# The triangular inverses of a chunked RWKV-7 recurrence: rows spread over the partitions, and one strict mask instead of two

## Chip, core and metric

One core of one Trainium2 chip runs the whole kernel in one launch. The metric is the device time of an execution in microseconds. Of three runs of the kernel before the median is 1870.58 us (1870.54 to 1880.12).

## What is computed

One layer of a decoder trunk on 1024 tokens of 1024 channels, all in float32: an input projection feeds a sparse attention, an RWKV-7 time mixing and two gates; then come a cross-attention and a mixture of experts with their norms. The part that matters here is the time mixing, with 8 heads of 64 channels. The reference runs it token by token:

```
def step(S, inp):
    r_t, w_t, k_t, v_t, kk_t, a_t = inp
    S = (S * w_t[:, :, None, :]
         - jnp.einsum('bhij,bhj->bhi', S, kk_t)[..., None] * (kk_t * a_t)[:, :, None, :]
         + v_t[..., None] * k_t[:, :, None, :])
    return S, jnp.einsum('bhij,bhj->bhi', S, r_t)
```

## The kernel before, in words

**The stage.** The input projection multiplies blocks of 128 weight columns with the 1024 tokens, each as three matmuls of split operands (lines 35 to 37: high by high, low by high, high by low). While these run, class Rwkv works through 8 items: 4 pairs of heads (hp) by 2 halves of 512 tokens (n). The string ORDER (line 1784) gives the order in which projection blocks of the recurrence ("r"), items ("i") and the other projection blocks ("b") are written; all items stand before the first "b". The framework then plans the order of each engine's instructions from a simulated timeline (line 1913), so the engines' queues interleave items with projections. Every engine runs its queue in order; a late operand holds up all that is behind it.

**An item** (`steps`, line 704) cuts the 512 tokens into 8 chunks of 64 for each of 2 heads. A pair of chunks shares a 128 x 128 tile, so there are 8 units u (2 heads by 4 pairs).

- Line 805: products of decayed keys and factors, four per bank of the PSUM tag tp, two banks' worth in use.
- Lines 809 to 814, for each of 4 banks: four instructions on 32 partitions cut the strictly triangular 32 x 32 diagonal blocks into lx (line 811), then three instructions on 128 partitions by 256 elements make f, lk and lo with the masks 0, 1 and 2. lk holds the strict triangles of the key half only; the other half of its 128 rows is zero. lo holds the off-diagonal 32 x 32 blocks.
- Line 836: per unit one product of lk with the values vt, 128 rows by 128 columns by 64, into rr.
- Lines 842 to 848: the blocks lx go to a memory tile ld (four stores) and come back as ln (four loads), so that each of the 32 blocks (8 units by 4) lies in one partition, four times: partition group g of 32 works on 8 of the 32 rows of each inverse.
- Lines 849 to 852: the inversion by substitution, 31 steps of two VectorE instructions, all over 8 rows and 31 - j elements. Group g holds rows 8g to 8g + 7; the identity is loaded into x first (line 846).
- Lines 855 to 859: the inverses x go to memory (xd, four stores), and come back as diagonal blocks of dt (four loads).
- Lines 866 to 881: for each head, TensorE applies dt, lo and dt again (line 870, its rhs is rr, z or qq in turn), with copies and sums on VectorE (z at line 873, w at 878, yv at 881) and ScalarE (qq at 876) between.
- Lines 885 to 894: products of f with w in 64 x 64 form (line 891), into gp.
- Lines 898 to 910: the chain over 8 chunks (lines 903 and 905, copies of the state at 909). Norm and gate follow in the next item's time (lines 913 to 939).

All transfers are issued on SyncE's queue, in its order: the four ld stores, the identity, the four ln loads, the four xd stores and the four dt loads of an item, between the weights' loads (line 114) and the evictions of the projections. A float32 product with float32 operands appears as two TensorE instructions in the profile, so line 836 has 16 per item.

Of the kernel before, what the change touches and what calls it, by code (L numbers as in the profile page):

```python
# [11 lines left out]
ALU = mybir.AluOpType  # L12
# [7 lines left out]
class Ctx:  # L20
    def __init__(self, tc, a):
        self.tc, self.nc, self.a = tc, tc.nc, a
        self.s = {}
# [587 lines left out]
def host_consts3():  # L611
    r = np.arange(128)[:, None] % 64
    t = np.arange(64)[None, :]
    lo_half = (np.arange(128) < 64)[:, None]
    incl, strict = (r <= t), (r < t)
    off = (r < 32) & (t >= 32)
    mk = np.zeros((4, 128, 2, 64), np.float32)
    for par in range(2):
        beta = lo_half if par == 0 else ~lo_half
        mk[0, :, par] = np.where(incl, np.where(beta, -1.0, 1.0), 0.0)  # L620
        mk[1, :, par] = strict & ~beta
        mk[2, :, par] = -1.0 * (off & beta)
        mk[3, :, par] = strict
    blk = (np.arange(128)[:, None] // 64 == np.arange(128)[None, :] // 64).astype(np.float32)
    sm = np.ones((128, 512), np.float32)
    sm[:, ::64] = 0
    return {"c_rmask": np.ascontiguousarray(mk.transpose(1, 0, 2, 3)), "c_blk": blk, "c_scan": sm,
            "c_i64": np.concatenate([np.eye(64, dtype=np.float32)] * 2, 0),
            "c_i32": np.repeat(np.eye(32, dtype=np.float32).reshape(4, 256), 32, 0)}


class Rwkv:
# [5 lines left out]
    def __init__(self, k, cst, dp, p1, pb, ps):  # L638
        self.k, self.cst, self.dp, self.p1, self.pb, self.ps = k, cst, dp, p1, pb, ps
        nc, a, s = k.nc, k.a, k.s  # L640
        s["or"], s["bo"] = ([dp.tile([128, T], F32, name=f"{n}{b}") for b in range(4)] for n in ("or", "bo"))

        def cload(name, shape, src):
            t = p1.tile(shape, F32, name=name)
            nc.sync.dma_start(t, src)
            return t
        self.rmask = cload("rmask", [128, 4, 2, 64], a["c_rmask"])
        self.blk = cload("blk", [128, 128], a["c_blk"])
        self.scan = cload("scan", [128, 512], a["c_scan"])
        self.i64 = cload("i64", [128, 64], a["c_i64"])  # L650
        vec = {}
        for n in ("w0", "a0", "kk", "ka", "gn_g", "gn_b"):
            vec[n] = cload("v" + n, [128, 4], a["rwkv_" + n][0].rearrange("(b p) -> p b", p=128))
        vec["rk"] = cload("vrk", [128, 4], a["rwkv_rk"][0].rearrange("(b h) d -> (h d) b", h=2))
        for n in ("w0", "a0"):
            nc.vector.tensor_scalar(vec[n], vec[n], 0.5, None, ALU.mult)
        vec["ka2"] = p1.tile([128, 4], F32, name="ka2")
        nc.vector.tensor_scalar(vec["ka2"], vec["ka"], -0.5, 1.0, ALU.mult, ALU.add)
        nc.vector.tensor_scalar(vec["ka"], vec["ka"], 0.5, None, ALU.mult)
        self.vec = vec  # L660
        self.mhalf = p1.tile([128, 8], F32, name="mhalf")
        nc.vector.memset(self.mhalf, -0.5)
        self.last, self.marks = (), {}
        self.dt = p1.tile([128, 8, 128], F32, name="dt")
        nc.gpsimd.memset(self.dt, 0.0)
        self.st = [p1.tile([128, 128], F32, name=f"state{i}") for i in range(2)]
        for t in self.st:
            nc.gpsimd.memset(t, 0.0)
# [35 lines left out]
    def steps(self, hp, n):  # L704
        k, nc, s, pb, ps, dp = self.k, self.k.nc, self.k.s, self.pb, self.ps, self.dp
        ident, rmask = self.cst["ident"], self.rmask
# [4 lines left out]
        def bank(tag="acc", bufs=2):  # L711
            return ps.tile([128, 512], F32, tag=tag, bufs=bufs, name="r" + tag)

        def big(tag, shape=(128, W), bufs=1):
            return pb.tile(list(shape), F32, tag=tag, bufs=bufs, name="r_" + tag)
# [24 lines left out]
        acc = bank("pa", 1)  # L740
        nc.tensor.matmul(acc, wa2[0:64], zwa[0:64], start=True, stop=True)
        nc.scalar.activation(th, acc, AF.Tanh, bias=v1["w0"], scale=0.5)
        acc = bank("pa", 1)
# [10 lines left out]
        acc = bank("pa", 1)  # L754
# [8 lines left out]
        acc = bank("pa", 1)  # L763
# [27 lines left out]
        acc = bank("pa", 1)  # L791
# [2 lines left out]
        nc.sync.dma_start(s["bo"][hp][:, ns], kx)  # L794

        f = big("f", (128, 2, 8, 2, 64), 3)
        lk, lo, lx = big("lk", (128, 8, 128)), big("lo", (128, 8, 128), 2), big("lx", (128, 8, 32))
        for h in range(2):
            rows = slice(64 * h, 64 * h + 64)
            for q in range(2):  # L800
                acc = bank("tp", 2)
                for i in range(4):
                    c = 4 * q + i
                    lhs = bk[rows, c // 2, 2 * (c % 2):2 * (c % 2) + 2, :].rearrange("p a t -> p (a t)")
                    nc.tensor.matmul(acc[:, 128 * i:128 * i + 128].rearrange("p (a t) -> p a t", a=2), lhs, ar[rows, 0:2, 64 * c:64 * c + 64], start=True, stop=True)
                a5 = acc.rearrange("p (c l x t) -> p c l x t", c=2, l=2, x=2)
                mb = lambda m: rmask[:, m].unsqueeze(1).to_broadcast([128, 2, 2, 64])
                us = slice(4 * h + 2 * q, 4 * h + 2 * q + 2)
                for b in range(4):
                    p2, t2 = slice(32 * b, 32 * b + 32), slice(32 * (b % 2), 32 * (b % 2) + 32)  # L810
                    nc.vector.tensor_tensor(lx[p2, us], a5[p2, :, b // 2, 0, t2], rmask[p2, 3, 0:1, t2].to_broadcast([32, 2, 32]), ALU.mult)
                nc.vector.tensor_tensor(f[:, h, 4 * q:4 * q + 4, 0, :].rearrange("p (c l) t -> p c l t", l=2), a5[:, :, :, 1, :], mb(0), ALU.mult)
                for m, dst in ((1, lk), (2, lo)):
                    nc.vector.tensor_tensor(dst[:, us].rearrange("p c (l t) -> p c l t", l=2), a5[:, :, :, 0, :], mb(m), ALU.mult)

        rr = big("rr", (128, 2, 8, 64))
        vt = big("vt", (128, 4, 2, 64))
# [15 lines left out]
            nc.scalar.copy(vt[h2], a4[o2])  # L833
        acc = bank("tp", 2)
        for u in range(8):
            nc.tensor.matmul(acc[:, 64 * u:64 * u + 64], lk[:, u], vt[:, u % 4, u // 4], start=True, stop=True)
        nc.scalar.copy(rr[:, 1], acc.rearrange("p (u i) -> p u i", i=64))

        ld = dp.tile([8, 4, 32, 32], F32, tag="ld", bufs=2, name="ld")
        xd = dp.tile([8, 4, 32, 32], F32, tag="xd", bufs=2, name="xd")  # L840
        for b in range(4):
            nc.sync.dma_start(ld[:, b].rearrange("u s t -> s u t"), lx[32 * b:32 * b + 32])

        ln = pb.tile([128, 32, 32], F32, tag="ln", name="ln")
        x, tmp = (pb.tile([128, 8, 32], F32, tag=m, name=m) for m in ("xinv", "tinv"))
# [1 line left out]
        for g in range(4):  # L847
            nc.sync.dma_start(ln[32 * g:32 * g + 32].rearrange("p s t -> p (s t)"), ld.rearrange("u b s t -> (u b) (s t)"))
        for j in range(31):
            w = 31 - j  # L850
            nc.vector.tensor_tensor(tmp[:, :, :w], x[:, :, j:j + 1].to_broadcast([128, 8, w]), ln[:, j:j + 1, j + 1:].to_broadcast([128, 8, w]), ALU.mult)  # L851
            nc.vector.tensor_tensor(x[:, :, j + 1:], x[:, :, j + 1:], tmp[:, :, :w], ALU.subtract)  # L852
        xv = xd.rearrange("u b (g s) t -> g (u b) (s t)", g=4)
        for g in range(4):
            nc.sync.dma_start(xv[g], x[32 * g:32 * g + 32].rearrange("p s t -> p (s t)"))
        dt = self.dt
        for b in range(4):
            bs = slice(32 * b, 32 * b + 32)
# [2 lines left out]
        w = big("w", (128, 8, 64))  # L861
# [4 lines left out]
        for h in range(2):  # L866
# [12 lines left out]
            for par in range(2):  # L879
                p2 = slice(64 * par, 64 * par + 64)  # L880
# [4 lines left out]
        for par in range(2):  # L885
            p2 = slice(64 * par, 64 * par + 64)
            acc = bank()
            for i in range(4):
                c = par + 2 * i
# [8 lines left out]
        for c in range(8):  # L898
            op = slice(64 * (c % 2), 64 * (c % 2) + 64)
            st, sn = self.st[c % 2], self.st[1 - c % 2]  # L900
            acc = bank("seq", 1)
# [24 lines left out]
        acc = bank()  # L926
# [9 lines left out]
        acc = bank()  # L936
# [536 lines left out]
class Experts:  # L1473
# [194 lines left out]
    def list(self, r, s0):  # L1668
        main = self.rows(self.pl, s0, "m")
        return main, self.rows(self.pl, s0 + CAP, "r", True) if r < NREM else None  # L1670
# [224 lines left out]


_CONSTS = [host_consts, host_consts2, host_consts3, host_consts5]


# [19 lines left out]
```

## Time and profile before

| what | value |
|---|---|
| median of three runs | 1870.58 us |
| the profiled execution | 1872.08 us |
| its span, first to last instruction | 1870.3 us |
| mean granted TensorE clock | 0.964 |
| busy TensorE / VectorE / ScalarE / GpSimd | 93% / 68% / 45% / 29% |

The granted clock is a share of 2.4 GHz, with two levels in this profile, 1.0 and 0.5. Busy time is the union of an engine's instructions. A wait is idle time of an engine directly ahead of an instruction, put down to what released it last. The recurrence occupies about the stretch from 150 to 650 us.

### The profile page before, as it was taken

How to read it: one execution, taken by the hardware profiler on the slowest of the kernel's cores; microseconds unless marked ns; L12 is line 12 of the kernel's file. 1: busy time of each engine (PE TensorE's matmuls, PEld its weight loads, DVE VectorE, ACT ScalarE, POOL GpSimd, SP SyncE). 2: the span in 40 equal slices, each digit the busy share in tenths (PEclk: the TensorE clock that was granted, in tenths of full speed). 3: DMA queues.
4: the chain of work that ended last, by engine and by line, in shares of the span. 5: the costliest groups of instructions: out<-in, count | busy, mean ns of one | idle time of the engine just before them, and what ended most of it. 6: DMA issues, size and time to landing. Idle time of an engine off the chain costs nothing. (4 is left out here: it accounts for less than half of the span.)

```text
span 1870.3 us, 27135 instructions
## 1 busy us (share of the span) xinstructions
PE 1744.0 (93%) x9126; PEld 1423.5 (76%) x9126; DVE 1277.4 (68%) x2866; ACT 845.5 (45%) x1756; POOL 535.9 (29%) x681
## 2 busy tenths in 40 slices
PE   8999998999999899999999789999998999999992
PEld 6877777777687787878888567878797888888871
DVE  3226876888877621489888575647887777777786
ACT  4233313433333222188888441015313676676672
POOL 1124202221211121166756222100015333333214
PEclk9999999999999899999999899999988999999996
DMA  7363343444432225811200675131433999998974
GB/s 232 113 187 109 108 167 117 131 131 121 112 109 80 78 85 172 275 57 39 84 10 21 200 232 189 46 99 52 162 135 125 326 291 298 294 306 299 310 273 152
DMA packets 245629, 296.01 MB, mean 158 GB/s; under 512 B 55597, under 2 KB 143685, under 8 KB 244976
## 3 DMA queue, kind: packets, MB, share of 16 engines
q1 hardware_dynamic: 238016, 273.59, 44.6%
q0 software_dynamic: 7472, 20.67, 4.5%
q8 instruction: 73, 1.20, 0.3%
q14 instruction: 68, 0.56, 0.1%
HBM read 231.95 MB, written 70.98 MB: 162 GB/s over the span
## 5 line engine op out<-in xcount | busy, mean ns | idle before, releaser
L35 PE MATMUL acc<-xh,wh 128*128 128x512 f32 (+1 forms) x656 | 272.6, 416 | 5.4 <-ACT wh L117 2.5
L37 PE MATMUL acc<-xh,wl 128*128 128x512 f32 (+1 forms) x656 | 266.8, 408 | 0.2 <-POOL wl L118 0.2
L36 PE MATMUL acc<-xl,wh 128*128 128x512 f32 (+1 forms) x656 | 266.2, 406 | 0.0
L1530 DVE TENSOR_TENSOR wlo<-wraw,whi 128x512 fp32r<-128x512 f32 x384 | 237.4, 683 | 30.0 <-ACT whi L1529 30.0
L1529 ACT CAST whi<-wraw 128x512 fp32r<-128x512 f32 x384 | 206.3, 621 | 19.2 <-issue 16.6
L118 POOL TENSOR_TENSOR wl<-wraw,wh 128x1024 fp32r<-128x1024 f32 (+1 forms) x41 | 100.9, 2462 | 304.4 <-ACT wh L117 250.8
L35 PEld LDWEIGHTS acc<-xh,wh 128*128 128x128 f32 (+1 forms) x656 | 125.1, 191 | 43.5 <-issue 5.5
L37 PEld LDWEIGHTS acc<-xh,wl 128*128 128x128 f32 (+1 forms) x656 | 124.5, 190 | 33.3 <-issue 4.7
L36 PEld LDWEIGHTS acc<-xl,wh 128*128 128x128 f32 (+1 forms) x656 | 124.7, 190 | 29.7 <-issue 3.2
L851 DVE TENSOR_TENSOR tinv<-xinv,ln 128x248 f32<-128x248 f32 (+30 forms) x248 | 91.4, 368 | 41.8 <-DMA ln<-ld 16.6
L475 ACT ACTIVATE pp<-pp,nm 128x640 f32<-128x640 f32 (+7 forms) x128 | 94.2, 739 | 9.3 <-DVE nm L474 8.1
L28 DVE TENSOR_TENSOR pl<-ptp,ph 128x512 fp32r<-128x512 f32 x132 | 87.3, 684 | 11.9 <-ACT ph L28 11.3
L35 PE MATMUL eacc<-whi,exh 128*128 128x512 f32 x240 | 94.2, 392 | 0.0
L36 PE MATMUL eacc<-wlo,exh 128*128 128x512 f32 x240 | 94.1, 392 | 0.0
L37 PE MATMUL eacc<-whi,exl 128*128 128x512 f32 x240 | 93.9, 391 | 0.0
L1638 POOL DMA_INDIRECT accd<-ey,ef x32 | 52.6, 1642 | 141.6 <-ACT ey L1633 60.1
L480 POOL TENSOR_SCALAR pp<-pp,wgt 128x640 f32<-128x640 f32 (+7 forms) x128 | 88.2, 715 | 0.6
L852 DVE TENSOR_TENSOR xinv<-xinv,tinv 128x248 f32<-128x248 f32 (+30 forms) x248 | 83.4, 336 | 5.9
L980 POOL TENSOR_SCALAR lnrs<-lnmv 128x1 f32<-128x1 f32 x21 | 18.0, 859 | 223.5 <-DVE lnmv L979 204.5
L28 ACT CAST ph<-ptp 128x512 fp32r<-128x512 f32 x132 | 73.8, 583 | 16.8 <-PE ptp L534 16.0
L534 PE MATMUL ptp<-ident,pp 128*128 128x128 f32 x528 | 79.2, 276 | 0.4 <-DVE pl L28 0.3
L909 ACT COPY state<-rseq 64x64 f32<-64x64 f32 x128 | 26.7, 208 | 115.9 <-PE rseq L905 96.8
(498 smaller groups left out, 4414.7 us busy)
## 6 DMA issues: line engine op xcount, KB each, us to landing
wraw<-in_moe_w_up SPq DMA_DIRECT2D x32, 1024.0 KB
wraw<-in_moe_w_gate SPq DMA_DIRECT2D x32, 1024.0 KB
wraw<-in_moe_w_down SPq DMA_DIRECT2D x32, 1024.0 KB
wraw<-in_w_in SPq DMA_DIRECT2D x40, 512.0 KB
sm<-ev SPq DMA_DIRECT2D x32, 256.0 KB
sr<-ev SPq DMA_DIRECT2D x28, 256.0 KB
skew<-skew SPq DMA_DIRECT2D x1, 4608.0 KB
xraw<-in_x SPq DMA_DIRECT2D x8, 512.0 KB
```

Source lines behind the costliest of these rows:

```text
L28: x = nc.scalar.copy(hi, src), (nc.gpsimd if by_pool else nc.vector).tensor_tensor(lo, src, hi.bitcast(F32), ALU.subtract)
L35: nc.tensor.matmul(out, ah, bh, start=start, stop=False)
L36: nc.tensor.matmul(out, ah, bl, start=False, stop=False)
L37: nc.tensor.matmul(out, al, bh, start=False, stop=stop)
L118: nc.gpsimd.tensor_tensor(wl, raw, wh.bitcast(F32), ALU.subtract)
L475: nc.scalar.activation(pt[:, :n], pt[:, :n], AF.Exp, bias=nm, scale=-1.0, accum_out=sums[:, 0, i:i + 1])
L480: nc.gpsimd.tensor_scalar(st[br, i][:, :n], st[br, i][:, :n], w[:, 0, i:i + 1], 1.0, ALU.mult, ALU.mult)
L534: nc.tensor.transpose(tp[:, 128 * i:128 * i + 128], st[br, i][:, c0:c0 + 128], ident)
L851: nc.vector.tensor_tensor(tmp[:, :, :w], x[:, :, j:j + 1].to_broadcast([128, 8, w]), ln[:, j:j + 1, j + 1:].to_broadcast([128, 8, w]), ALU ...
L852: nc.vector.tensor_tensor(x[:, :, j + 1:], x[:, :, j + 1:], tmp[:, :, :w], ALU.subtract)
L1529: nc.scalar.copy(hi[:, cs], raw[:, cs])
L1530: (nc.gpsimd if i in LOPOOL else nc.vector).tensor_tensor(lo[:, cs], raw[:, cs], hi[:, cs].bitcast(F32), ALU.subtract)
```

## The change

1. The inversion. Partition group g now holds rows g, g + 4, g + 8, ... of each inverse (the identity constant is laid out accordingly). At step j only rows up to j can have a nonzero element in column j, so only the first m = j // 4 + 1 rows held per partition are touched. The stores of xd write rows of 32 elements at a step of four rows.
2. The masks. Mask 1 becomes the full strict triangle; lx, its four instructions per bank and mask 3 go. lk, now first of three, serves both the keys' product and the blocks stored to ld.
3. The keys' product. As the other half of lk is no longer zero, line 836's product becomes two per unit, each with 64 rows and 64 columns.

```
-    mk = np.zeros((4, 128, 2, 64), np.float32)
+    mk = np.zeros((3, 128, 2, 64), np.float32)
...
-        mk[1, :, par] = strict & ~beta
+        mk[1, :, par] = strict
         mk[2, :, par] = -1.0 * (off & beta)
-        mk[3, :, par] = strict
...
-            "c_i32": np.repeat(np.eye(32, dtype=np.float32).reshape(4, 256), 32, 0)}
+            "c_i32": np.repeat(np.eye(32, dtype=np.float32).reshape(8, 4, 32).transpose(1, 0, 2).reshape(4, 256), 32, 0)}
...
-        lk, lo, lx = big("lk", (128, 8, 128)), big("lo", (128, 8, 128), 2), big("lx", (128, 8, 32))
+        lk, lo = big("lk", (128, 8, 128)), big("lo", (128, 8, 128), 2)
...
-                for b in range(4):
-                    p2, t2 = slice(32 * b, 32 * b + 32), slice(32 * (b % 2), 32 * (b % 2) + 32)
-                    nc.vector.tensor_tensor(lx[p2, us], a5[p2, :, b // 2, 0, t2], rmask[p2, 3, 0:1, t2].to_broadcast([32, 2, 32]), ALU.mult)
-                nc.vector.tensor_tensor(f[:, h, 4 * q:4 * q + 4, 0, :].rearrange("p (c l) t -> p c l t", l=2), a5[:, :, :, 1, :], mb(0), ALU.mult)
                 for m, dst in ((1, lk), (2, lo)):
                     nc.vector.tensor_tensor(dst[:, us].rearrange("p c (l t) -> p c l t", l=2), a5[:, :, :, 0, :], mb(m), ALU.mult)
+                nc.vector.tensor_tensor(f[:, h, 4 * q:4 * q + 4, 0, :].rearrange("p (c l) t -> p c l t", l=2), a5[:, :, :, 1, :], mb(0), ALU.mult)
...
-            nc.tensor.matmul(acc[:, 64 * u:64 * u + 64], lk[:, u], vt[:, u % 4, u // 4], start=True, stop=True)
+            for l in range(2):
+
+                ls, ks = slice(64 * l, 64 * l + 64), slice(64 - 64 * l, 128 - 64 * l)
+                nc.tensor.matmul(acc[ls, 64 * u:64 * u + 64], lk[ks, u, ls], vt[ks, u % 4, u // 4], start=True, stop=True)
...
-            nc.sync.dma_start(ld[:, b].rearrange("u s t -> s u t"), lx[32 * b:32 * b + 32])
+            nc.sync.dma_start(ld[:, b].rearrange("u s t -> s u t"), lk[32 * b:32 * b + 32, :, 32 * b:32 * b + 32])
...
-            w = 31 - j
-            nc.vector.tensor_tensor(tmp[:, :, :w], x[:, :, j:j + 1].to_broadcast([128, 8, w]), ln[:, j:j + 1, j + 1:].to_broadcast([128, 8, w]), ALU.mult)
-            nc.vector.tensor_tensor(x[:, :, j + 1:], x[:, :, j + 1:], tmp[:, :, :w], ALU.subtract)
-        xv = xd.rearrange("u b (g s) t -> g (u b) (s t)", g=4)
+            w, m = 31 - j, j // 4 + 1
+            nc.vector.tensor_tensor(tmp[:, :m, :w], x[:, :m, j:j + 1].to_broadcast([128, m, w]), ln[:, j:j + 1, j + 1:].to_broadcast([128, m, w]), ALU.mult)
+            nc.vector.tensor_tensor(x[:, :m, j + 1:], x[:, :m, j + 1:], tmp[:, :m, :w], ALU.subtract)
+        xv = xd.rearrange("u b (s g) t -> g (u b) s t", g=4)
         for g in range(4):
-            nc.sync.dma_start(xv[g], x[32 * g:32 * g + 32].rearrange("p s t -> p (s t)"))
+            nc.sync.dma_start(xv[g], x[32 * g:32 * g + 32])
```

## Rows read from the trace of the kernel before

**Rows 1.** The page, part 1: busy us of each engine (share of the span) xinstructions.
```profile
PE 1744.0 (93%) x9126; PEld 1423.5 (76%) x9126; DVE 1277.4 (68%) x2866; ACT 845.5 (45%) x1756; POOL 535.9 (29%) x681
```

**Rows 2.** Busy us by stretch: PE, PEld, DVE, ACT, POOL, then PEclk, DMA share, GB/s.
```profile
150.00:650.00 500.00, 468.23 (x2645) 373.18 (x2645) 393.97 (x1049) 169.19 (x366) 108.87 (x82) 0.96 0.38 115
...
655.00:790.00 135.00, 132.18 (x712) 109.62 (x711) 37.07 (x77) 31.18 (x73) 25.88 (x13) 1.00 0.59 182
```

**Rows 3.** TensorE's waits, 150 to 650 us: line <- released by: total us, times, longest.
```profile
PE racc L870 <- DVE r_z L873: 6.7, 5, 1.9
PE racc L870 <- DMA dt<-xd: 5.5, 3, 2.7
PE racc L891 <- DVE r_w L878: 4.8, 1, 4.8
PE rpa L765 <- DVE r_cs L761: 4.7, 3, 2.7
...
PE rtp L805 <- DVE r_lo L814: 1.1, 1, 1.1
PE rtp L822 <- DVE xinv L852: 1.0, 1, 1.0
...
PE acc L35 <- DVE ev L199: 0.9, 1, 0.9
```

**Rows 4.** VectorE's groups, 150 to 650 us: xcount, busy us, mean ns, idle before.
```profile
L851 DVE TENSOR_TENSOR tinv<-xinv,ln 128x248 f32<-128x248 f32 (+30 forms) x248 | 91.4, 368 | 41.8 <-DMA ln<-ld 16.6 <-DMA sm<-ev 8.4 <-DMA sks1h<-ev 7.5
L852 DVE TENSOR_TENSOR xinv<-xinv,tinv 128x248 f32<-128x248 f32 (+30 forms) x248 | 83.4, 336 | 5.9
L811 DVE TENSOR_TENSOR r_lx<-rtp,rmask 32x64 f32<-32x64 f32 x128 | 28.0, 218 | 7.0 <-PE rtp L805 5.1
```

**Rows 5.** VectorE's timeline at 183 and from 630 us: start us, us, instruction.
```profile
183.15 0.42 DVE L851 TENSOR_TENSOR tinv<-xinv,ln 128x248 f32<-128x248 f32 x1 [1.33 <-DMA ln<-ld]
...
630.60 2.42 DVE L851 TENSOR_TENSOR tinv<-xinv,ln 128x72 f32<-128x72 f32 x1
...
639.17 0.17 DVE L852 TENSOR_TENSOR xinv<-xinv,tinv 128x8 f32<-128x8 f32 x1
```

**Rows 6.** Busy us of three stretches at half clock, columns as in rows 2.
```profile
431.40:434.80 3.40, 3.40 (x15) 3.21 (x15) 2.56 (x7) 1.17 (x2) 0.00 (x0) 0.50 0.56 106
509.90:513.30 3.40, 3.40 (x12) 2.79 (x10) 3.25 (x12) 1.59 (x3) 0.80 (x1) 0.50 0.32 95
...
632.70:646.40 13.70, 10.75 (x49) 7.73 (x49) 7.51 (x27) 1.34 (x4) 0.23 (x1) 0.50 0.21 53
```

**Rows 7.** TensorE's timeline beside them; the brackets give the wait before.
```profile
431.13 1.26 PE L870 MATMUL racc<-r_z,r_lo 128*128 128x128 f32 x5 [0.97 <-DVE r_z L873]
...
508.44 1.16 PE L870 MATMUL racc<-r_z,r_lo 128*128 128x128 f32 x8 [1.85 <-DVE r_z L873]
...
635.65 1.97 PE L891 MATMUL racc<-r_f,r_w 64*64 64x128 f32 x14 [4.81 <-DVE r_w L878]
```

**Rows 8.** TensorE's timeline at 192 and 257 us: lines 836 and 891, merged runs.
```profile
192.23 1.90 PE L836 MATMUL rtp<-r_vt,r_lk 128*128 128x64 f32 x16
...
257.17 0.39 PE L36 MATMUL acc<-xl,wh 128*128 128x512 f32 x1
257.40 0.40 PE L37 MATMUL acc<-xh,wl 128*128 128x512 f32 x1
257.73 1.58 PE L891 MATMUL racc<-r_f,r_w 64*64 64x128 f32 x30
```

**Rows 9.** SyncE's timeline: the trip of ld at 483 us, of xd at 524 us.
```profile
483.66 1.85 SPq L842 DMA_DIRECT2D ld<-r_lx  x4
486.74 1.71 SPq L848 DMA_DIRECT2D ln<-ld  x4
...
524.07 1.72 SPq L855 DMA_DIRECT2D xd<-xinv  x4
...
526.99 1.80 SPq L859 DMA_DIRECT2D dt<-xd  x4
```

More of the change, by code (lines that the diff above doesn't have):

```diff
@@ L646, in cload @@
             return t
-        self.rmask = cload("rmask", [128, 4, 2, 64], a["c_rmask"])
+        self.rmask = cload("rmask", [128, 3, 2, 64], a["c_rmask"])
         self.blk = cload("blk", [128, 128], a["c_blk"])
```

## The prediction

> **What bounds the kernel now.** The engine totals come first [rows 1]: TensorE is busy 93% of the span, VectorE 68%. Averages hide the stages, so I next read the stretch in which the recurrence runs, 150 to 650 us, beside the one behind it, where the same projections go on without the inversions [rows 2]. In the first TensorE is busy 468.2 of 500 us, idle 31.8 us or 6.4%, with VectorE at 394 us; in the second it is idle 2.8 of 135 us, 2.1%, with VectorE at 37 us. So TensorE bounds both, and what the recurrence can still give is the idle time that it causes, not its own length. The waits of TensorE say who ends that idle time [rows 3]: the six rows that name a VectorE result (r_z, r_w, r_cs, r_lo, the inversion, an eviction) sum to 6.7 + 4.8 + 4.7 + 1.1 + 1.0 + 0.9 = 19.2 us; the block inverses coming back from memory (dt) make 5.5 us. VectorE's groups show what stands in its queue [rows 4]: the two instructions of the inversion take 91.4 + 83.4 = 174.8 us and the lx masks 28.0 us, 203 of its 394 us, nearly all of it waited for by nobody but the recurrence itself.
>
> **The inversion.** Its 62 instructions per item stay; their sizes fall. Step j now runs over j // 4 + 1 rows of 31 - j elements instead of 8 rows. Summed over the 31 steps that is 1560 elements instead of 8 x 496 = 3968. One instruction of 248 elements took 0.42 us, one of 8 took 0.17 [rows 5]: 0.25 us for 240 elements, 1.04 ns each, on a fixed part of about 0.16 us. Saved per item: 2 x 2408 x 1.04 ns = 5.0 us, over 8 items 40 us. By the same line the old inversions should have taken 8 x (62 x 0.16 + 7936 x 0.00104) = 145 us; the other 30 us of the 174.8 are instructions that stalled, as the one of 72 elements that took 2.42 us where the line gives 0.23 [rows 5]. I leave those stalls in.
>
> **The masks.** The 128 lx instructions go: 28.0 us [rows 4]. The lk and lo masks keep their size, the f mask only moves behind them. Together VectorE loses 40 + 28 = 68 of 394 us in this stretch; its load falls from 0.79 to 326 / 500 = 0.65.
>
> **What TensorE gets of it.** None of this is TensorE work, so the 68 us count only through the 19.2 us of waits. Bounds: nothing, since the order on each engine is planned from assumed durations and a plan with shorter inversions can place the dependent matmuls earlier by as much; and all 19.2 us. In between I take a queue estimate: an instruction that arrives at a server with load u waits in proportion to u / (1 - u), 3.76 before and 1.86 after, half. As the plan will use up some of this, I take 40%: 7.7 us. It lies nearer the estimate than to nothing because the largest wait is just this: TensorE stood 4.81 us before the w product [rows 7] while VectorE worked through steps of the inversion, one of them stalled [rows 5].
>
> Some of these waits have a second price. Stretches in which TensorE was granted half its clock (1.2 of 2.4 GHz) begin right behind or inside a VectorE wait at 431.4, 509.9 and 632.7 us [rows 6, 7]. In them TensorE was busy 3.40 + 3.40 + 10.75 = 17.6 us, which at full clock is 8.8 us of work, so they cost 8.8 us. If 40% of their causes go, 3.5 us goes. Bounds: nothing, and 8.8 us.
>
> **The keys' product.** One product with 128 rows becomes two of 64 rows and 64 columns: 32 instructions per item instead of 16. The old ones came every (1.90 - 0.28) / 15 = 0.108 us, and the nearest rows to the new form, the 64 x 64 products of line 891, every (1.58 - 0.27) / 29 = 0.045 us [rows 8]. So 32 x 0.045 = 1.4 us stands against 16 x 0.108 = 1.7 us. From the last projection matmul to the first 64 x 64 one passed 257.73 - 257.40 = 0.33 us, where two projections followed each other after 0.23 [rows 8]; two such 0.1 us per item eat the difference. I take zero. Bounds: -0.3 us per item, and 32 x 0.108 - 1.7 = +1.8 us per item, 14 us in all, if the pairs do not overlap. The Trainium skill (TensorEngine Tiling (Array Packing), Key Properties) speaks against the change here: it says that a change of the tiling mode drains the engine. It gives no size, so by it the sum would only be worse; by the rows it is 8 x 2 x 0.1 = 1.6 us against 2.4 us gained, so the drain is seen and is small.
>
> **The transfers.** ld now leaves from lk: still 32 partitions x 8 runs of 128 bytes per store, as the block is 32 elements wide; zero. The stores now wait for the last lk instead of the last lx; lk is the first of three masks behind each bank, about 0.42 us as an instruction of this size took [rows 5], where four lx of 0.22 us stood first [rows 4], so they start no later. xd is written as runs of 128 bytes instead of 1 KB per partition, 256 runs a store. The nearest rows are the ld stores, which have these runs: from the end of their four issues to the first load behind them passed 486.74 - (483.66 + 1.85) = 1.23 us; for the 1 KB runs of xd 526.99 - (524.07 + 1.72) = 1.20 us, and issuing four took 1.85 against 1.72 us [rows 9]. So about 0.1 to 0.2 us per item, on the path from an inversion to dt. It is covered by projection matmuls where TensorE has them planned before line 870; the cover is gone where TensorE already waits for dt, three times now [rows 3], so under 0.5 us: zero. Behind the stores on SyncE's queue stand dt's loads and weights, shifted by the same 0.1 us. The smaller mask load and the lost lx tile cost nothing: no wait names either.
>
> **The sum.** -7.7 - 3.5 = -11.2 us. The profiled execution took 1872.1 us (span 1870.3), 1.5 us above the median of the runs, 1870.6; the terms apply to either, so the forecast is 1870.6 - 11.2 = 1859.
>
> **Rivals.**
> - *No change.* VectorE was not the bound and the plan spends the shorter inversions: TensorE's DVE waits stay near 19 us, with other names. For it: the order of work is planned, and TensorE is 94% busy. Against it: half of VectorE's work in this stretch shrinks, and the waits come where its queue is long. Time about 1868, between 1863 and 1873.
> - *Slower: dt takes the place.* The plan puts line 870's products earlier because the inversion is shorter, but the two trips through memory stay, so TensorE stands for dt in all 8 items instead of 3. Price: five more waits of the longest now, 2.7 us [rows 3], each followed by a half-clock stretch of 3.4 us like those of [rows 6], 1.7 us lost: 5 x 4.4 = 22 us, less the 11 gained: 1881. It decides from three such items on. Against it: the trips measured with 128 byte runs are no longer than with 1 KB. The Trainium skill (DMA: Bandwidth & Descriptors, Specifications) speaks for it: transfers under 512 bytes are read-modify-written and lose line rate; by it the trips lengthen and this rival comes, by [rows 9], where no such difference shows, the forecast does.
> - *Far more.* All VectorE waits go, and the half-clock stretches with them: -19.2 - 8.8 = -28 us, 1843. For it, the waits are short, mean 1 to 2 us. Against it, stalls like the 2.42 us one remain.
> - *The pairs do not overlap* (+14 us): 1859 + 14 = 1873. Against it: 0.045 us on line 891.
>
> **How the numbers follow.** A measurement of this kernel can tell about 0.5%, 9.4 us, from no change: faster is below 1861.2, slower above 1880. Forecast 0.42 (1852 to 1865; 0.36 of it counts as faster), no change 0.22, slower by dt 0.18 (0.14 of it above 1880), far more 0.12, no overlap 0.06. Faster 0.36 + 0.12 = 0.48; same 0.06 + 0.22 + 0.04 + 0.06 = 0.38; slower 0.14. The likeliest case by itself spans 1852 to 1865. The range runs from 1845 to 1879; it leaves out half of the far more case and most of the slower one.
>
> **What would show it.** Right: in 150 to 650 us VectorE near 326 us, the inversion near 135 us, no lx; TensorE's waits on VectorE near 11 us; fewer half-clock stretches; line 836's 256 instructions in about 12 us. Wrong: the dt row of the waits above 11 us, line 836 above 20 us, or the same sum of VectorE waits under other names. As TensorE has no other work to lose, an equal idle time there would mean that VectorE's saving went nowhere.

## The result, and the profile after

Before took 1873.16 us and the changed kernel 1857.49 us (medians of 16 runs each): a ratio of 0.9923, 95% interval 0.9910 to 0.9935, so 0.8% faster, 15.7 us between the medians. The profiled execution of after took 1859.28 us, its span 1857.5 us.

The rows of the profile after that answer to those of before. First the engine totals, against [rows 1]:

```profile
PE 1740.5 (94%) x9254; PEld 1419.5 (76%) x9254; DVE 1203.8 (65%) x2738; ACT 845.1 (45%) x1756; POOL 534.5 (29%) x681
```

TensorE has 128 instructions more (the split product), VectorE 128 fewer (the lx masks) and 74 us less to do. Then the two stretches of [rows 2], columns as there:

```profile
150.00:650.00 500.00, 483.86 (x2943) 384.53 (x2943) 327.17 (x940) 176.29 (x387) 116.36 (x88) 0.97 0.40 119
655.00:790.00 135.00, 131.34 (x673) 108.62 (x671) 40.90 (x114) 38.41 (x100) 27.62 (x32) 0.97 0.60 190
```

VectorE's load in the recurrence is 327 us where it was 394, and TensorE's idle time in those 500 us fell from 31.8 to 500 - 483.86 = 16.1 us. VectorE's groups, against [rows 4]:

```profile
L850 DVE TENSOR_TENSOR tinv<-xinv,ln 128x60 f32<-128x60 f32 (+24 forms) x248 | 66.9, 270 | 23.0 <-DMA ln<-ld 16.6
L851 DVE TENSOR_TENSOR xinv<-xinv,tinv 128x60 f32<-128x60 f32 (+24 forms) x248 | 62.9, 253 | 6.4
```

The inversion takes 66.9 + 62.9 = 129.8 us instead of 174.8. TensorE's waits from 120 to 720 us, against [rows 3] (in that longer stretch before has the same rows for VectorE):

```profile
PE rseq L902 <- DVE r_yv L880: 3.7, 2, 3.2
...
PE acc L35 <- DVE ev L227: 1.6, 1, 1.6
PE racc L927 <- DVE r_ot L924: 1.5, 1, 1.5
...
PE rpa L791 <- DVE r_r L789: 1.2, 1, 1.2
...
PE acc L35 <- DVE ev L28: 0.9, 1, 0.9
PE acc L35 <- DVE ev L199: 0.9, 2, 0.8
PE rseq L904 <- DVE xinv L851: 0.8, 1, 0.8
PE racc L869 <- DMA dt<-xd: 0.6, 1, 0.6
PE rtp L804 <- DVE r_bk L779: 0.3, 1, 0.3
PE rpa L740 <- DVE r_k L792: 0.3, 1, 0.3
```

The nine rows that name VectorE sum to 11.2 us (before 19.6: the prediction's six rows of 19.2 leave out one of 0.4 us for r_k, line 793); r_z, r_w, r_cs and r_lo are no longer among them, and the wait for dt fell from 5.5 to 0.6 us. Last the split product and the transfers of one item, on TensorE's and on SyncE's timeline, against [rows 8, 9]:

```profile
193.47 0.27 PE L764 MATMUL rpa<-ident,r_cs 128*128 128x128 f32 x1
193.67 1.15 PE L835 MATMUL rtp<-r_vt,r_lk 64*64 64x64 f32 x32
```

```profile
491.03 2.51 SPq L854 DMA_DIRECT2D xd<-xinv  x4
...
494.97 1.81 SPq L858 DMA_DIRECT2D dt<-xd  x4
```

32 instructions of 64 x 64 take 1.15 us where 16 of 128 rows took 1.90. The four xd stores take 2.51 us to issue instead of 1.72, and the trip behind them 494.97 - 493.54 = 1.43 us instead of 1.20. Over all eight items the medians are 2.51 against 1.74 us for issuing, and 1.45 against 1.27 us for the trip.

**Where the time went.** Three marks divide every kernel here in the same way: the first attention score product on TensorE (up to there projections and recurrence run), the first matmul of the first expert, and the end of the span.

| us | attention starts | TensorE busy / idle until then | time at 1.2 GHz until then | attention to first expert | first expert to end |
|---|---|---|---|---|---|
| before | 796.8 | 752.7 / 44.1 | 41.0 | 622.5 | 451.0 |
| after | 774.1 | 745.0 / 29.1 | 37.5 | 628.5 | 454.9 |
| difference | -22.7 | -7.7 / -15.0 | -3.5 | +6.0 | +3.9 |

Busy and idle come from this row of each trace (columns of [rows 2]), of before and of after:

```profile
0.00:796.80 796.80, 752.67 (x4084) 606.29 (x4085) 480.17 (x1218) 253.20 (x528) 170.03 (x128) 0.97 0.45 137
```

```profile
0.00:774.10 774.10, 745.00 (x4213) 596.37 (x4214) 404.51 (x1090) 252.92 (x528) 168.20 (x128) 0.98 0.46 141
```

So the stage gained 22.7 us, and 9.9 us of it were lost behind it, where nothing was edited. The loss in the last column has a visible place at the first expert, whose activations are gathered by the router's lists. TensorE transposes the gathered rows (line 1564, after 1563). TensorE's timeline there, before and then after:

```profile
1431.80 1.12 PE L1564 MATMUL etp<-ident,exg 128*128 128x128 f32 x4 [6.68 <-DMA exg<-x2d,ef]
1434.31 0.79 PE L1597 MATMUL eacc<-whi,exr 128*128 128x512 f32 x1 [1.40 <-DVE exr L28]
...
1441.57 1.03 PE L1564 MATMUL etp<-ident,exg 128*128 128x128 f32 x8
```

```profile
1413.23 1.12 PE L1563 MATMUL etp<-ident,exg 128*128 128x128 f32 x4 [4.48 <-DMA exg<-x2d,ef]
1422.31 1.94 PE L1563 MATMUL etp<-ident,exg 128*128 128x128 f32 x8 [7.97 <-DMA exg<-x2d,ef]
1423.90 0.78 PE L1596 MATMUL eacc<-whi,exr 128*128 128x512 f32 x1
```

Before, TensorE's queue holds four transposes of the first gather, then the products of the remainder (exr), then eight transposes of the second gather, which has arrived by then. After, the twelve transposes stand in a row, and the products behind them wait as TensorE waits for the second gather: 7.97 us more. I call these order A and order B. The edit touches neither; the planned order came out differently.

### The profile page after: what moved, and what is told of

Its sections match the earlier page's. It is cut to its first block, busy times and chain, and to the rows that moved or that the text cites. A ratio compares the mean times of both kernels' runs of the same rounds, so it can differ in the third digit from the quotient of the medians.

```text
span 1857.5 us, 27257 instructions
## 1 busy us (share of the span) xinstructions
PE 1740.5 (94%) x9254; PEld 1419.5 (76%) x9254; DVE 1203.8 (65%) x2738; ACT 845.1 (45%) x1756; POOL 534.5 (29%) x681
## 5 line engine op out<-in xcount | busy, mean ns | idle before, releaser
L35 PE MATMUL acc<-xh,wh 128*128 128x512 f32 (+1 forms) x656 | 268.1, 409 | 8.4 <-ACT wh L117 3.3
L35 PEld LDWEIGHTS acc<-xh,wh 128*128 128x128 f32 (+1 forms) x656 | 124.2, 189 | 44.1 <-ACT wh L117 4.2
L117 ACT CAST wh<-wraw 128x1024 fp32r<-128x1024 f32 (+1 forms) x41 | 42.3, 1031 | 87.2 <-PE acc L36 43.1
L850 DVE TENSOR_TENSOR tinv<-xinv,ln 128x60 f32<-128x60 f32 (+24 forms) x248 | 66.9, 270 | 23.0 <-DMA ln<-ld 16.6
L28 ACT CAST ph<-ptp 128x512 fp32r<-128x512 f32 x132 | 73.7, 581 | 16.6 <-PE ptp L534 15.6
```

Source lines behind the costliest of these rows:

```text
L28: x = nc.scalar.copy(hi, src), (nc.gpsimd if by_pool else nc.vector).tensor_tensor(lo, src, hi.bitcast(F32), ALU.subtract)
L35: nc.tensor.matmul(out, ah, bh, start=start, stop=False)
L850: nc.vector.tensor_tensor(tmp[:, :m, :w], x[:, :m, j:j + 1].to_broadcast([128, m, w]), ln[:, j:j + 1, j + 1:].to_broadcast([128, m, w]), A ...
```

## The experiments

My theory at this point: the recurrence's VectorE chain is what TensorE waited for, and what the shorter chain gave was partly returned by order B. Its rivals: the gain comes from a part to which I had given nothing (the split product, the order of the masks), or from the accident of a new plan, or differs between executions by that much. The runs came from several chips, on which before had medians from 1873 to 1882 us, so a total is compared as a ratio with runs of before on the same chip. The marks of all runs, each from one trace:

| | attention starts | TensorE busy / idle | at 1.2 GHz | attention to first expert | first expert to end | order | ratio [95%] |
|---|---|---|---|---|---|---|---|
| before_again | 796.2 | 751.7 / 44.5 | 37.5 | 633.5 | 448.7 | A | one run |
| after_again | 778.2 | 748.4 / 29.8 | 44.4 | 630.7 | 455.8 | B | one run |
| order_only | 794.6 | 750.3 / 44.3 | 37.5 | 630.3 | 446.7 | A | 0.9983 [0.9964, 1.0002] |
| inv_only | 794.5 | 754.9 / 39.6 | 58.0 | 630.8 | 455.7 | B | 1.0008 [0.9990, 1.0025] |
| product_only | 782.7 | 744.7 / 38.0 | 34.1 | 627.5 | 457.0 | B | 0.9939 [0.9922, 0.9956] |
| product_order | 782.6 | 747.1 / 35.5 | 41.0 | 628.3 | 454.6 | B | one run |
| inv_product | 786.2 | 745.6 / 40.6 | 37.5 | 634.8 | 455.6 | B | 1.0021 [0.9999, 1.0043] |
| mask_only | 784.6 | 742.7 / 41.9 | 30.7 | 631.1 | 451.4 | A | 0.9914 [0.9885, 0.9942] |
| no_steps | 746.8 | 731.2 / 15.6 | 17.1 | 625.5 | 449.3 | A | one run |
| double_steps | 858.1 | 780.8 / 77.3 | 119.5 | 633.7 | 458.3 | B | one run |
| hold | 772.8 | 743.1 / 29.7 | 30.7 | 628.0 | 456.7 | held | 0.9860 [0.9834, 0.9885] |
| hold_again | 774.1 | 745.6 / 28.5 | 37.5 | 625.9 | 458.0 | held | 0.9912 [0.9881, 0.9943] |

**before_again and after_again** are the two kernels unchanged, once more with a profile.

> The kernel before, unchanged, profiled once more: how far one profile's markers move by themselves. The start of the attention within 1 us of 796.8 us and TensorE's idle time before it within 2 us of 37.4 us if these follow from the program; by several us if they are chance of an execution, and then no difference of that size between kernels means anything.

> The changed kernel, unchanged, on the same chip as the run before it. Start of the attention within 1 us of 774.1 us. The stretch from there to the end was 1073.5 us before and 1083.4 us after: if the 10 us that the change lost again there belong to the program, they show once more beside the run of the kernel before; if they were chance of an execution, the two stretches agree within 4 us.

They took 1880.17 and 1866.44 us. The same program repeats the attention mark within 0.6 us (before) and 4.1 us (after); the difference of the two kernels there is -18.0 us this time, -14.7 of it idle time. From attention to the first expert before took 622.5 us once and 633.5 once, with the same instructions in the same queues. So the +6.0 us of the first table in that stretch is scatter of single executions: the second pair has -2.8 there. What repeats is the last column: +3.9 and +7.1 us.

**order_only** puts only the f mask behind the other two.

```
-                nc.vector.tensor_tensor(f[:, h, 4 * q:4 * q + 4, 0, :].rearrange("p (c l) t -> p c l t", l=2), a5[:, :, :, 1, :], mb(0), ALU.mult)
                 for m, dst in ((1, lk), (2, lo)):
...
+                nc.vector.tensor_tensor(f[:, h, 4 * q:4 * q + 4, 0, :].rearrange("p (c l) t -> p c l t", l=2), a5[:, :, :, 1, :], mb(0), ALU.mult)
```

> Nothing is removed: the f mask moves behind lk and lo, as in the change. Queue theory: same VectorE work, start of the attention within 3 us of 796.8 us, the whole within 0.2%. Luck of the plan: the start of the attention or the total moves by over 5 us (0.3%), and then a part of the full change's gain can't be put down to VectorE's saved work.

Measured 1877.96 us against 1882.19, a ratio whose interval touches 1, and 2.2 us at the attention mark. A new plan by itself moved little here.

**inv_only** has the new layout of rows, the shorter steps and the new xd stores, with the old masks and product.

```
...
-            w = 31 - j
+            w, m = 31 - j, j // 4 + 1
...
```

> The inversion's part alone: every fourth row per partition, only the reached rows, xd stored in 128-byte runs; masks, lx and the keys' product as before. Queue theory (TensorE's idle time follows VectorE's load): VectorE loses about 40 us in 150 to 650 us, the attention's first score matmul comes 10 to 15 us before the 796.8 us of the kernel before, the whole 0.4 to 0.7% faster. Rival, luck of the plan (any re-timed order moves TensorE's waits by as much): the start of the attention moves by up to 10 us either way without regard to the 40 us. Rival, short runs: dt waits of TensorE rise above the 5.5 us of before.

Measured 1883.55 us against 1882.19: nothing. The row up to the attention mark:

```profile
0.00:794.50 794.50, 754.91 (x4084) 606.72 (x4085) 437.69 (x1218) 252.62 (x528) 167.16 (x128) 0.96 0.45 137
```

VectorE lost 42.5 us of work and TensorE 4.5 us of idle time; but TensorE was busy 2.2 us longer, with 58.0 us at 1.2 GHz instead of 41.0. Among its waits are two that before did not have in this size (waits of TensorE, 120 to 720 us):

```profile
PE rpa L741 <- DMA r_k<-z: 6.1, 2, 5.1
PE acc L35 <- DVE ev L199: 5.3, 1, 5.3
```

In sum TensorE's waits on VectorE are 14.9 us, where before had 19.6. From the first expert on the kernel takes 455.7 us, with order B.

**product_only** splits line 836 on the kernel before, whose lk has the zero half; the half is not read.

```
-            nc.tensor.matmul(acc[:, 64 * u:64 * u + 64], lk[:, u], vt[:, u % 4, u // 4], start=True, stop=True)
+            for l in range(2):
+
+                ls, ks = slice(64 * l, 64 * l + 64), slice(64 - 64 * l, 128 - 64 * l)
+                nc.tensor.matmul(acc[ls, 64 * u:64 * u + 64], lk[ks, u, ls], vt[ks, u % 4, u // 4], start=True, stop=True)
```

> Only the keys' product is split into two of 64 rows and 64 columns (the half of lk that is zero is no longer read); masks and inversion as before. Queue theory: VectorE's work is the same, the start of the attention within 3 us of 796.8 us, the whole within 0.2%. Rival, the products pay: 256 instructions at about 63 ns instead of 128 at 112 ns give or take 2 us. Luck of the plan: over 5 us either way.

Measured 1871.71 us, 0.6% faster, the interval well clear of 1. The row up to the mark, and TensorE's group of the product (150 to 650 us) in before and then here:

```profile
0.00:782.70 782.70, 744.70 (x4212) 597.03 (x4213) 474.86 (x1218) 253.45 (x528) 169.74 (x128) 0.98 0.46 139
```

```profile
L836 PE MATMUL rtp<-r_vt,r_lk 128*128 128x64 f32 x128 | 16.2, 277 | 1.5 <-ACT r_vt L833 1.5
```

```profile
L839 PE MATMUL rtp<-r_vt,r_lk 64*64 64x64 f32 x256 | 11.9, 245 | 0.6 <-ACT r_vt L833 0.6
```

The attention mark moved by 14.1 us, of which 16.2 - 11.9 = 4.3 us are the product itself; 6.1 us are idle time, though the edit takes no instruction from VectorE (it was busy 474.9 us up to the mark, 480.2 before). Between them they leave 3.7 us, of which a part is the lower clock, held for 34.1 us instead of 41.0. TensorE's waits on VectorE show where the idle time changed (120 to 720 us, against [rows 3]):

```profile
PE rseq L906 <- DVE r_yv L884: 5.4, 1, 5.4
...
PE racc L873 <- DVE r_z L876: 2.5, 2, 1.4
...
PE racc L894 <- DVE r_w L881: 1.5, 2, 1.4
...
PE rpa L765 <- DVE r_cs L761: 1.3, 1, 1.3
```

The waits for r_z and r_cs shrink from 6.7 + 4.7 = 11.4 to 3.8 us, that for r_w from 4.8 to 1.5, and one of 5.4 us for r_yv is new; in sum VectorE's rows fall from 19.6 to 13.1 us. Why a product that is shorter by 4.3 us takes more than its own length out of these waits is not shown by any run.

**product_order** is product_only and order_only together: another plan with the same product.

> The split product, and the f mask behind lk and lo: two edits that leave VectorE's work as before, another order of the plan. If the split product's 14 us at the start of the attention belong to it (shorter products, and what waits for them), the start is within 4 us of 782.7 us. If they are luck of one plan, it lies elsewhere, between 785 and 800 us, only the 4 us of shorter products being left.

The attention mark came at 782.6 us against 782.7, one run of 1867.36 us beside before's 1877.28. So the 14 us are no accident of one plan. In all six kernels here that split the product and run every step of the inversion the mark lies at 786.2 us or earlier; in the three that do not split it and add no work it lies at 794.5 us or later.

**inv_product** is inv_only and product_only together: all of the change but the masks.

> The inversion's part and the split product together, the masks and lx as before. If the parts add up (inversion alone -2.3 us, product alone -14.1 us at the start of the attention), it starts at about 780 us, the total 0.6% faster. If VectorE's load is what counts once another order is planned, as between the masks' part with product (784.6 us) and the full change (774.1 us), it comes 10 us before the product alone, near 772 us, 1% faster. Luck of the plan: anywhere between 770 and 800 us.

Measured 1882.17 us against 1878.94: not faster. The mark stands at 786.2 us, 3.5 us later than with the product alone, though VectorE had 36.9 us less to do. The parts do not add up. Here the plan puts the xd stores of one item behind the transfer of line 293, a copy of 4608 KB, on SyncE's queue, and in after it puts them ahead of it. SyncE's timeline, inv_product and then after:

```profile
252.48 0.74 SPq L293 DMA_DIRECT2D skew<-skew  x1
254.43 16.61 SPq L858 DMA_DIRECT2D xd<-xinv  x4
```

```profile
253.35 2.52 SPq L854 DMA_DIRECT2D xd<-xinv  x4
...
267.12 0.73 SPq L293 DMA_DIRECT2D skew<-skew  x1
```

Behind the copy the four stores take 16.61 us to issue, and TensorE then stands for their dt:

```profile
285.38 2.05 PE L873 MATMUL racc<-r_rr,dt 128*128 128x128 f32 x8 [7.48 <-DMA dt<-xd]
```

In inv_only the stores of that item stand behind the same copy and take 11.47 us, and so does the load of r_k, for which TensorE waits 5.1 us. By these traces a part of what the shorter inversion did not give in the two kernels is a matter of places in SyncE's queue. No run moves the copy, so how much is not shown.

**mask_only** is the complement of inv_only: one strict mask, no lx, split product, with the old steps and layout.

> The masks' part alone: one strict mask, no lx, the keys' product as two of 64 rows; the inversion over 8 rows as before. Queue theory: VectorE loses about 28 us, the attention starts 7 to 11 us earlier, the whole 0.2 to 0.5% faster; with the inversion's part it adds up to the 22.7 us that the full change has there. Luck of the plan: it does not add up, one part alone may show all of it or a loss.

```profile
0.00:784.60 784.60, 742.68 (x4212) 595.98 (x4213) 452.38 (x1090) 253.43 (x528) 171.09 (x128) 0.98 0.45 139
```

Measured 1866.44 us against 1882.19, 0.9914: the interval overlaps that of the full change, 0.9923. Its attention mark comes 10.5 us later than the full change's, but it gets order A, and its last column stays at before's level, 451.4 us. Beside product_only, with 22.5 us less of VectorE work, its mark is 1.9 us later: at the mark the masks give nothing on top of the product until the shorter inversion is there too. The masks without the split product were not run.

**no_steps** shortens the inversion of the changed kernel to its first step; **double_steps** does the multiply of each step of the old inversion twice. Both ask how TensorE's idle time follows VectorE's work. As no_steps leaves the inverses out, all behind it gets other values, and only the stage up to the mark is read.

```
-        for j in range(31):
+        for j in range(1):
```

```
-            nc.vector.tensor_tensor(tmp[:, :, :w], x[:, :, j:j + 1].to_broadcast([128, 8, w]), ln[:, j:j + 1, j + 1:].to_broadcast([128, 8, w]), ALU.mult)
+            for _ in range(2):
+                nc.vector.tensor_tensor(tmp[:, :, :w], x[:, :, j:j + 1].to_broadcast([128, 8, w]), ln[:, j:j + 1, j + 1:].to_broadcast([128, 8, w]), ALU.mult)
```

> The full change with only the first of the 31 inversion steps: the inverses are left out, so what follows gets other values (the routing too, so only the stage before the attention is read). VectorE loses some 125 us more. If TensorE's idle time follows VectorE's load: TensorE's waits on VectorE fall from 12 us to under 4 us, the attention starts at 760 to 766 us. If what is left of the idle time is a matter of the planned order and of ScalarE and transfers: the start stays within 6 us of 776 us.

> A dose of VectorE work: in the kernel before each multiplication of the inversion is issued twice (same result), 91 us more on VectorE. Queue theory: load in 150 to 650 us near 0.95, TensorE's waits on VectorE well above the 20 us of before, 40 us or more, the attention starting over 20 us later than 796.8 us. If VectorE's load does not bind TensorE (the plan puts other projections in between), the start moves by less than 8 us.

The rows up to the mark, no_steps and then double_steps:

```profile
0.00:746.80 746.80, 731.17 (x4212) 591.02 (x4213) 295.09 (x610) 252.93 (x528) 166.63 (x128) 0.99 0.47 146
```

```profile
0.00:858.10 858.10, 780.78 (x4084) 626.66 (x4085) 548.12 (x1466) 252.78 (x528) 169.44 (x128) 0.93 0.41 127
```

VectorE's work up to the mark and TensorE's idle time, in us:

| VectorE | idle | kernels |
|---|---|---|
| 295 | 15.6 | no_steps |
| 404 | 28.5 to 29.8 | after, after_again, hold, hold_again |
| 438 | 39.6, 40.6 | inv_only, inv_product |
| 452 | 41.9 | mask_only |
| 474, 475 | 35.5, 38.0 | product_order, product_only |
| 478 to 480 | 44.1 to 44.5 | before, before_again, order_only |
| 548 | 77.3 | double_steps |

Over the whole range idle time rises with VectorE's work. Between 438 and 480 us it does not follow it: it lies between 35.5 and 44.5 us, and the lowest values come with 474 and 475 us of work, from two kernels with the split product. In double_steps TensorE waits for dt itself, once for 15.0 us, and the lower clock lasts three times as long as before:

```profile
PE racc L871 <- DMA dt<-xd: 23.9, 4, 15.0
```

So VectorE's chain can bind TensorE, but within the change the amount of its work does not tell what a part gives. Against mask_only, the inversion's part in the full change moves the mark by 10.5 us (6.4 by after_again) and the total by nothing that shows (0.9923 against 0.9914). no_steps shows what is left of the inversion: 27.3 us at the mark.

**hold and hold_again** are the changed kernel with the transposes of the second gather held behind the last matmul of the first remainder product of the first expert, to restore order A: the framework then issues them after it. The second is a repeat on another chip.

```
...
-        for q in range(0 if first else 2):
-            k.split(self.turned(ps, main[2], q).rearrange("p (c t) -> p c t", c=4), xh[:, 4 * q:4 * q + 4], xl[:, 4 * q:4 * q + 4])
+        with ExitStack() as st:
+            if self.mark:
+                st.enter_context(k.tc.issue_after(self.mark))
+                self.mark = None
+            for q in range(0 if first else 2):
+                k.split(self.turned(ps, main[2], q).rearrange("p (c t) -> p c t", c=4), xh[:, 4 * q:4 * q + 4], xl[:, 4 * q:4 * q + 4])
...
-                    nc.tensor.matmul(o, xr[:, c], wt[c // 4][j][:, c % 4], start=c + j == 0, stop=c + j == 8)
+                    m = nc.tensor.matmul(o, xr[:, c], wt[c // 4][j][:, c % 4], start=c + j == 0, stop=c + j == 8)
+            if first and i == 0:
+                self.mark = m.ins
```

> The full change, and TensorE's transposes of the second expert's gathered rows held behind the first remainder product of the first expert. Theory (the gain is given back at the first expert, where the order of the plan puts those transposes 4 us after a gather that takes until 20 us): the wait of 8 to 10 us for the second gather shrinks to about 3 us, the stretch from the first expert matmul to the end takes 449 to 451 us instead of 455 us, the total 4 to 6 us below the full change, ratio to before about 0.988 to 0.990. Rival (the transfers of the expert weights are what is late, and some wait follows wherever the transposes stand): the stretch stays at 455 us, the ratio at 0.992. The start of the attention stays at 774 to 778 us in both.

> The kernel with the held transposes, unchanged, once more: its one profile fell on the slowest of its five runs, 1859.3 us, with the first gather issued 12.6 us behind the first expert matmul and a wait of 13.2 us. If the hold is worth some 6 us beyond the full change, the ratio to before is 0.984 to 0.989 again, and a profile near the median shows waits for gathers of 8 us or less in sum and 449 to 452 us from the first expert matmul to the end. If the 0.986 was chance, the ratio comes out near the 0.992 of the full change.

```profile
1420.06 1.11 PE L1564 MATMUL etp<-ident,exg 128*128 128x128 f32 x4 [13.18 <-DMA exg<-x2d,ef]
1422.57 0.80 PE L1601 MATMUL eacc<-whi,exr 128*128 128x512 f32 x1 [1.40 <-DVE exr L28]
...
1427.69 1.03 PE L1564 MATMUL etp<-ident,exg 128*128 128x128 f32 x8
```

TensorE's order is that of before again, and there is one wait instead of two. But the first gather now lands later, the one wait is 13.18 us, and the last column stays at 456.7 and 458.0 us. What delays it stands on the timeline of GpSimd, which issues the gathers, beside that of VectorE (hold):

```profile
1408.27 4.98 POOL L1549 TENSOR_TENSOR ef<-ef 128x1 f32<-128x1 f32 x1
1413.41 1.06 POOL L1557 DMA_INDIRECT exg<-x2d,ef  x1
```

```profile
1408.32 4.89 DVE L1530 TENSOR_TENSOR wlo<-wraw,whi 128x512 fp32r<-128x512 f32 x8
```

An addition whose median in this trace is 0.2 us took 4.98 us while VectorE split eight blocks of expert weights, and the first gather was issued behind it. In hold_again the gather's own instruction took 5.62 us beside the same eight. In both, and in every kernel with order B, these eight start 7.4 to 7.6 us after the first matmul of the first expert; with order A VectorE's splits start there after 11.1 us or more, when the first two gathers have been issued or are being issued. So the hold restored the order of TensorE's queue and not that of VectorE's: whether TensorE's order alone makes the loss is not tested by it. In all runs the last column goes with the sum of TensorE's waits for these gathers: 2.1 to 6.7 us with order A (446.7 to 451.4 us to the end), 11.3 to 14.6 with order B (454.6 to 458.3), 13.2 and 13.4 here. The two ratios, 0.9860 and 0.9912, have intervals that barely touch, and the second overlaps that of the full change: whether this version is faster than the change is not settled, and its traces show no gain in the stretch that it edits.

## Why the prediction was right in its number, and not in its reasons

The forecast was 1859 us and the measured median 1857.49. Against before's median beside it, 1873.16, the gain is 15.7 us, where 11.2 were forecast. Step by step:

- **The inversion and the masks**: VectorE near 326 us in the stretch, measured 327.2; the inversion near 135, measured 129.8 (45.0 us saved where 40 were forecast); lx gone. The line through two sizes and the decision to leave the stalls in both held.
- **What TensorE gets of it**: TensorE's waits on VectorE near 11.5 us, measured 11.2. That number came out, but the step "none of this is TensorE work, so the 68 us count only through the 19.2 us of waits" named too small a pool. Idle time until the attention mark fell by 15.0 us and 14.7 in the second pair. In the first 8.4 us of it are in the VectorE rows and 4.9 in the dt row, in the second 6.8 and 3.1; the dt row I had costed at zero as unaffected. Why it fell is not shown: it is 0.6 us in after, but 3.1 in inv_only and 7.9 in inv_product, which have the same shorter inversion, and 1.8 in mask_only, which has the old one.
- **The cause of it**: here the prediction fell. The inversion alone gives 1.0008, with the product 1.0021; the masks and the product without it give as much as the whole change, 0.9914. VectorE's work moves TensorE's idle time over a wide range (295 to 548 us, 15.6 to 77.3), but 42 us of it bought 4.5 us of idle time in inv_only. Of these 2.3 us were left at the mark, where TensorE was busy longer with more time at 1.2 GHz, and nothing in the total. The step that failed is to take VectorE's load, by u / (1 - u), for the measure of these waits: between 438 and 480 us of work the idle time does not follow it, and in inv_product one wait for dt, behind a place on SyncE's queue, is 7.5 us.
- **The keys' product**: the term "I take zero" was mis-sized and is the one that failed most. Its own part is 16.2 - 11.9 = 4.3 us alone, and alone it moved the stage by 14.1 us; where the rest of the 14.1 us comes from stays open. My two extra 0.1 us per item do not show: in the rows of the item above the split product starts 0.20 us behind the transpose before it, and lasts 1.15 us against 1.90. Its 256 instructions, put at about 12 us, took 10.8 in after, whose group in the stretch from 150 to 650 us is

```profile
L835 PE MATMUL rtp<-r_vt,r_lk 64*64 64x64 f32 x256 | 10.8, 224 | 0.0
```

- **The clock**: -3.5 us was forecast. From the times at 1.2 GHz and the share in which TensorE was busy then, the loss went from 19.0 to 18.0 us, and in the second pair from 17.3 to 21.6: no gain. Before has nine such stretches up to the mark, of which the prediction priced three. Five of the nine begin behind or inside a VectorE wait and hold 27.3 us; in after two of five do, with 6.8 us. The others, behind waits for ScalarE's results or transfers, grew from 13.7 to 30.7 us, and that was not foreseen.
- **The xd stores**: 0.1 to 0.2 us per item were forecast, (2.51 - 1.72) + (1.43 - 1.20) = 1.0 us measured, 0.8 of it in issuing. The cover held in after all the same: its waits for dt are 0.6 us. The Trainium skill (DMA: Bandwidth & Descriptors, Specifications) has transfers under 512 bytes lose line rate. The trace agrees in sign, with a trip 0.23 us longer here. The rival named beside it did not come.
- **The change of the tiling mode**: the product became shorter in every kernel that splits it. The Trainium skill (TensorEngine Tiling (Array Packing), Key Properties) says that such a change drains the engine. No row here shows a cost of it that could be told apart.
- **Behind the stage**: the prediction looked at no wait outside the recurrence. Behind the first expert's first matmul 3.9 and 7.1 us went back, which go with the waits for the gathers there. So the number came out right by luck: a stage gain about twice as large as forecast (18 to 23 us against 11) met a loss that was not forecast.

The rivals: "no change" is excluded for the whole change by the interval, though for the inversion alone it is what came (1.0008); "dt takes the place" is excluded by 0.6 us, "the pairs do not overlap" by 1.15 us per item. "Far more" had a true core: waits and product together gave 18 to 23 us at the attention mark, but no clock.

## What to carry to other kernels

Where the queues' order is planned from the whole program, an edit changes work far behind it: compare marks along the span, not only the stage, and the queues of all engines, not only the one that waits, and profile both kernels twice before a difference of some us in an unedited stretch is explained. Run each part of a change alone and its complement, since parts that share a critical engine need not add up: here the part with the most saved work (42 us of VectorE) gave nothing alone, and taking the half that is zero out of one product gave 0.6%.

## What the runs showed of the hardware that I had not expected

- Here two products in 64*64 form were cheaper than the one in 128*128 form that holds both: 32 instructions in 1.15 us, 1.15 / 32 = 0.036 us each, against 1.90 / 16 = 0.119 us.
- Two executions of one program, before and before_again, were 11.0 us apart in a stretch of some 630 us (622.5 and 633.5), while the stage ahead of it repeated within 0.6 us (within 4.1 us for after and after_again).
- The time at 1.2 GHz up to the attention mark is 17.1 us with 15.6 us of idle time and 119.5 us with 77.3. In between it does not follow the idle time: 58.0 us with 39.6 (inv_only), 30.7 with 41.9 (mask_only).
- Issuing an xd store took SyncE longer with 128-byte runs (2.51 us for four) than with runs of 1 KB (1.72 us for four).
- Short instructions of VectorE and GpSimd were stretched beside longer work of the other: the step of 2.42 us in [rows 5], from 630.60 us, stands beside a GpSimd subtraction of 2.40 us (line 118, from 630.52 us), and hold's addition of 4.98 us beside 4.89 us of VectorE.
- Behind the copy of 4608 KB four xd stores took 16.61 us to issue (inv_product) and 11.47 us (inv_only), where each four of after took 2.51 to 2.65 us.
